# Moving stationary and moving tiles to other address differences modulo 512, and turning the order of three products in one stage

## The chip, the cores and the metric

The kernel runs on one core of a Trainium2 chip. The metric is the device time of one execution in microseconds. Before the change the median of two runs is 2041.47 us (2041.25 to 2041.7).

## What is computed

A decoder trunk of two layers for 256 tokens of width 2048, in float32, with 256 memory tokens. Cut to what matters:

```python
def layer_a(h, mem, ...):
    z = rms_norm(h, norm_attn) @ w_in                  # 2048 x (1536 + 1536 + 36 + 512)
    ... rope, native sparse attention (compressed, selected, window branches), memory attention
    h = h + concatenate([o_nsa, o_mem]) @ w_out        # 2048 x 2048
    return h + swiglu(rms_norm(h, norm_ffn), w_gate, w_up, w_down)   # d_ff = 5632

def reference(...):
    h = layer_a(x, mem, ...)
    kv = rms_norm(h, kv_norm) @ w_kv_shared            # 2048 x 1024
    ... layer_b: z = rms_norm(h, norm_attn) @ w_in     # 2048 x 2048
    ... dilated attention on the shared K and V, memory attention
    h = h + concatenate([o_dil, o_mem]) @ w_out        # 1024 x 2048
    h = h + swiglu(rms_norm(h, norm_ffn), w_gate, w_up, w_down)
    return rms_norm(h, final_norm)
```

`compress` in layer A's attention is a two-layer MLP over overlapping blocks of 32 tokens. The feed-forward parts are the largest matrix products.

## The kernel before

**Three products for one.** TensorE multiplies in the fp32r type. For accuracy each float32 operand is split into a high and a low part (`split`, lines 74 to 81: ScalarE makes the high part with a copy into fp32r, VectorE the low part as the difference). `mm3` then issues three matmuls into one PSUM tile: high by high (line 85), stationary low by moving high (line 86), stationary high by moving low (line 87). Its argument `l` is the stationary operand, 128 columns of activations that the array holds, and `r` the moving operand, up to 512 columns of weights that stream through. Each matmul instruction brings its own load of the stationary operand (LDWEIGHTS).

**Where the operands come from.** `load_w` brings a weight chunk by DMA on SyncE's queue into `raw` (pool `wp`, four buffers) and splits it into `whi` and `wlo` (three buffers each). `Gemm.part` runs `mm3` over the chunk's slices for one of the two halves of the tokens. Activations are split in advance and stay in SBUF: `xhi`/`xlo` (pool `xp`) hold the normalised input of a projection, `ohi`/`olo` (pool `pa`) the memory tokens and later the attention's output in layer A, `obhi`/`oblo` (pool `pc`) the attention's output in layer B, `hThi`/`hTlo` (pool `h`) the hidden activations of the feed-forward part.

**The feed-forward part** (`Group`, `run_groups`) multiplies the first six row blocks of the contraction in a Strassen form: quarters of the weights are loaded into `q11`, `q12`, `q22`, `q21`, combined by VectorE, split into `qhi` and `qlo` (pool `q`) and used by `product`; the other row blocks come as plain chunks through `load_w` (`plain`). So both `w` and `q` weights meet `x` (gate and up) and `hT` (down).

**Order.** TensorE's order is the order of the program text. `Side.tick` puts the smaller steps (transposes, attention products) between the slices of the large products at hand-written places. The other engines' order is left to the framework.

**Stages in time.** Memory K/V of both layers (stationary `o`), layer A's projections (stationary `x`, two of them in blocks of 274 columns), layer A's attention among its query projection, output projection (`o`), layer A's feed-forward part, layer B's shared K/V and query projections with its attention (`x`), output projection (`ob`), layer B's feed-forward part.

**Where tiles lie.** A pool's tiles stand one after the other, each buffer rounded up to 32 bytes per partition, and pools that are open together stand one after the other in the order of opening: constants, `wp`, `xp`, `small`, `work`, and then those of the phase (in layer A `ac`, `pa`, `p1` or `p2`; in the feed-forward phases `h` and `q`; in layer B's attention `acb` and `pc`). Some tiles exist only to move what follows (`padc`, `padw`, `pada`). Laid out so, `whi`, `wlo`, `xhi`, `xlo`, `ohi`, `olo`, `obhi`, `oblo`, `hThi`, `hTlo`, `qhi` and `qlo` all begin 224 bytes beyond a multiple of 512, and a 128-column slice of fp32r is 512 bytes long. So before the change every matmul with 512 columns has its stationary and its moving tile at difference 0 modulo 512. A slice of 274 columns is 1096 bytes, 72 beyond a multiple of 512, so in those blocks every second slice has another difference. In the compression MLP (lines 624 and 625) the stationaries are 60 columns, 240 bytes apart.

Of the kernel before, what the change touches and what calls it, by code (L numbers as in the profile page):

```python
# [8 lines left out]
F32 = mybir.dt.float32  # L9
# [7 lines left out]
P = 128  # L17
# [24 lines left out]
def decoder_trunk(ctx: ExitStack, tc: tile.TileContext, a: dict, out: bass.AP):  # L42
    nc = tc.nc

    const = ctx.enter_context(tc.tile_pool(name="const", bufs=1))
    wp = ctx.enter_context(tc.tile_pool(name="wp", bufs=4))
    dram = ctx.enter_context(tc.tile_pool(name="dram", bufs=1, space=bass.MemoryType.DRAM))
    xp = ctx.enter_context(tc.tile_pool(name="xp", bufs=1))
    small = ctx.enter_context(tc.tile_pool(name="small", bufs=6))
    work = ctx.enter_context(tc.tile_pool(name="work", bufs=1))  # L50
    work.tile([P, 20], F32, name="padw")
    phase = ctx.enter_context(ExitStack())
    aux_stack = ExitStack()
    fbufs = [1]
    fpool = mm_ps = aux_ps = mm_tags = None

    def open_phase(name, mms, auxs):
        nonlocal mm_ps, mm_tags, aux_ps
        mm_ps = phase.enter_context(tc.tile_pool(name="m" + name, bufs=1, space=PSUM))
        mm_tags = mms  # L60
        phase.enter_context(aux_stack)
        aux_ps = aux_stack.enter_context(tc.tile_pool(name="x" + name, bufs=auxs, space=PSUM))
# [17 lines left out]
            nc.vector.scalar_tensor_tensor(lo, src, gain, hi.bitcast(F32),  # L80
                                           op0=ALU.mult, op1=ALU.subtract)

    def mm3(o, l, r, start, stop, more=False):

        nc.tensor.matmul(o, l[0], r[0], start=start, stop=False, skip_group_check=more)  # L85
        nc.tensor.matmul(o, l[1], r[0], start=False, stop=False, skip_group_check=more)  # L86
        nc.tensor.matmul(o, l[0], r[1], start=False, stop=stop, skip_group_check=more)  # L87

    def pair(f):
        return f(0), f(1)  # L90
# [38 lines left out]
    class Gemm:  # L129
# [16 lines left out]
        def part(self, ws, tt, k0, side):  # L146
            for i, w in enumerate(ws):
                k = k0 + i
                x = self.xs[k](tt)
                mm3(self.ps[tt][:, :self.ncols], x, w, k == 0, k == self.nk - 1)  # L150
                side.tick()

    def cols(pr):
# [2 lines left out]
    def take(steps=()):  # L156
        got = deferred + list(steps)
        deferred.clear()
        return Side(got)

    def at(fs, *ticks):
        assert len(fs) == len(ticks)
        return list(zip(ticks, fs))
# [4 lines left out]
    def gemm(chunks, xs, ncols, nk, gain=None, steps=(), pre=None, first=None):  # L168
        side = take(steps)
        g = Gemm(chunks, xs, ncols, nk, gain)  # L170
        g.run(0, len(chunks), side, pre, first)
        side.flush()
        return g.ps

    def wblocks(name, nb, nchunk):
        w = a[name]
        return [[w[b, c] for c in range(nchunk)] for b in range(nb)]
# [27 lines left out]
    def finish_rstd(ssq, n):  # L205
        v = small.tile([P, 2], F32, tag="var", name="var")
        if n > 1:
            nc.vector.tensor_reduce(v, ssq, axis=AX.X, op=ALU.add)
        else:
            nc.vector.tensor_copy(v, ssq[:, :, 0])  # L210
        nc.vector.tensor_scalar(v, v, 1.0 / D, EPS, op0=ALU.mult, op1=ALU.add)
        r = small.tile([P, 2], F32, tag="rstd", name="rstd")
        nc.gpsimd.tensor_tensor(r, v, halfneg, op=ALU.pow)
        return r
# [5 lines left out]
    def new_ssq():  # L220
        return small.tile([P, 2, 4], F32, tag="ssq", name="ssq")
# [12 lines left out]
    def new_x():  # L234
        return pair(lambda i: xp.tile([P, XW], F32R, tag=("xhi", "xlo")[i], name=("xhi", "xlo")[i]))
# [85 lines left out]
    def residual_block(ps, nb, ssq, op, ticks=(3, 5)):  # L321
        for tt in range(2):
            hb = h[:, tt, nb * 512:(nb + 1) * 512]
            nc.vector.tensor_add(hb, ps[tt], hb)
            square_sum(ssq[:, tt, nb:nb + 1], hb)
        deferred.extend(at([lambda k2=k2: op.turn(nb, k2) for k2 in range(2)], *ticks))
# [66 lines left out]
    def mem_head(q, mkT, mv, hd, O):  # L393
        st = {}

        def scores():
            S = aux_tile()
            for qt in range(2):
                mm3(S[:, qt * T:(qt + 1) * T], sl(q, slice(None), slice(qt * P, (qt + 1) * P)),
                    sl(mkT, slice(None), hd, slice(None)), True, True)  # L400
            negm = small.tile([P, 2], F32, tag="mnegm", name="mnegm")
            den = small.tile([P, 2], F32, tag="mden", name="mden")
            nc.vector.tensor_reduce(negm, S.rearrange("p (q k) -> p q k", q=2), axis=AX.X, op=ALU.max, negate=True)
            E = new_E(512)
            for qt in range(2):
                exp_(E[:, qt * T:(qt + 1) * T], S[:, qt * T:(qt + 1) * T], negm[:, qt:qt + 1], den[:, qt:qt + 1])
            c = softmax_coef(den)
            for qt in range(2):
                nc.vector.tensor_scalar_mul(E[:, qt * T:(qt + 1) * T], E[:, qt * T:(qt + 1) * T], c[:, qt:qt + 1])
            st["E"] = E  # L410

        def turn():
            st["PT"] = new_PT("mPT")
            transposed([st["E"][:, qt * T + mt * P:qt * T + (mt + 1) * P] for mt in range(2) for qt in range(2)], st["PT"])

        def values():
            for mt in range(2):
                mm3(O(), sl(mv, slice(None), mt, slice(hd * P, (hd + 1) * P)),
                    sl(st["PT"], slice(None), slice(mt * T, (mt + 1) * T)), mt == 0, mt == 1)

        return scores, turn, values
# [20 lines left out]
    stack = ExitStack()  # L442
    pa = stack.enter_context(tc.tile_pool(name="pa", bufs=1))
    kv4 = [pa.tile([P, 1152], F32R, tag="kv4", name="kv4", bufs=4) for _ in range(4)]
    mkT_b = pair(lambda i: kv4[i][:, :1024].rearrange("p (c t) -> p c t", t=T))
    mv_b = pair(lambda i: kv4[2 + i][:, :1024].rearrange("p (c t) -> p c t", t=512))
    memkv = [dram.tile([P, 1024], F32, name=f"memkv{i}") for i in range(4)]
# [364 lines left out]
    def project_out(name, nk, ready, gi):  # L812
        op = Paired(new_x(), KT, lambda k: gains[:, gi, k:k + 1])
        ssq = new_ssq()
        ob = wblocks(name, 4, nk // CK)
        n = nk // CK
        side = take()
        g = [Gemm(ob[i], osx, 512, nk) for i in range(2)]
        side.rate = max(1, 8 / (2 * ready))
        for i in range(2):  # L820
            g[i].run(0, ready, side)
        side.flush()
        for i in range(2):
            side = take()
            g[i].run(ready, n, side)
            side.flush()
            residual_block(g[i].ps, i, ssq, op)
        for nb in range(2, 4):
            ps = gemm(ob[nb], osx, 512, nk)
            residual_block(ps, nb, ssq, op, (3, 5) if nb == 2 else (4, 10))  # L830
        return op, finish_rstd(ssq, 4)
# [198 lines left out]
    def open_ffn(name):  # L1030
        nonlocal fh, fq, fpool
        fbufs[0] = 2
        open_phase(name, FFN, 1)
        fh = phase.enter_context(tc.tile_pool(name="h" + name, bufs=1))
        fpool = fq = phase.enter_context(tc.tile_pool(name="q" + name, bufs=1))

    fh = fq = None
    open_ffn("fa")
    xb = None
    ssq_b = new_ssq()  # L1040
# [10 lines left out]
    phase.close()  # L1051

    open_phase("b", ATT, 4)
    ac = phase.enter_context(tc.tile_pool(name="acb", bufs=1))
    cs = ac.tile([P, 2, 2, HD], F32, name="cs")
    nc.gpsimd.dma_start(cs, a["cs"])
# [85 lines left out]
    for j in range(4):  # L1142
# [8 lines left out]
        deferred.extend(at(heads_T(tok, qT), 4, 7))  # L1151
        deferred.extend(at(dil_head(qT, j), 10, 13, 15, 20, 22, 25, 28, 30))
    fpool = pc
    fx, f_r = project_out("b_w_out", 8, 3, 6)
    stack.close()
    phase.close()
    open_ffn("fb")

    def final(db, hs, n):
# [137 lines left out]
def build(nc, arrays):  # L1297
    from concourse import tile as _tile

    aps = {}  # L1300
    import numpy as np
    for name, v in arrays.items():
        dt = BF16 if v.dtype.itemsize == 2 else mybir.dt.from_np(v.dtype)
        aps[name] = nc.dram_tensor(f"in_{name}_dram", v.shape, dt, kind="ExternalInput").ap()
    out = nc.dram_tensor("out_0_dram", (T, D), F32, kind="ExternalOutput").ap()
    with _tile.TileContext(nc) as tc:
        with tc.manual_schedule(engines={mybir.EngineType.PE}):
            decoder_trunk(tc, aps, out)
# [12 lines left out]
```

## Time and profile before

| | |
|---|---|
| Median of the runs | 2041.47 us |
| The profiled execution | 2041.91 us, span 2040.1 us |
| TensorE matmuls busy | 2020.5 us, 99%, 9417 instructions |
| Weight loads busy | 1676.7 us, 82%, 9417 instructions |
| VectorE busy | 1641.4 us, 80% |
| ScalarE busy | 1190.4 us, 58% |
| HBM read | 394.87 MB, 196 GB/s over the span |

Busy time of matmuls is a union of overlapping durations: one with 512 columns is shown with about 390 ns, while the next one starts much earlier. How fast TensorE goes is therefore read from the distance between starts in the timeline. PE is TensorE's matmul, PEld its weight load, DVE VectorE, ACT ScalarE, POOL GpSimd, SP SyncE. L85 is line 85 of the kernel; as `mm3` and `split` are helpers, the tile names tell which product a row belongs to.

### The profile page before, as it was taken

Reading aid. Unit: us, or ns where it says so; the run is one execution under the profiler, and the core shown is the slowest. Engines: PE = TensorE matmul, PEld = TensorE weight load, DVE = VectorE, ACT = ScalarE, POOL = GpSimd, SP = SyncE. Lnnn points to the kernel's source line nnn. Section 1 sums busy time; section 2 is a strip of 40 time slices with the busy share of each in tenths; the row PEclk is TensorE's granted clock in tenths of the full one; section 3 lists DMA queues with packets and bytes.
Section 4 is the critical chain, followed back from the end, with each engine's and each line's share of the span. In section 5 each row is a group of like instructions: output and inputs, shape, how many; then the busy total and the mean of one; then the engine's idle time right before and its main releaser. Section 6 shows DMA issues by size and latency. Waiting matters only on the chain.

```text
span 2040.1 us, 25602 instructions
## 1 busy us (share of the span) xinstructions
PE 2020.5 (99%) x9417; PEld 1676.7 (82%) x9417; DVE 1641.4 (80%) x2118; ACT 1190.4 (58%) x1573; POOL 10.8 (1%) x32
## 2 busy tenths in 40 slices
PE   9999999999999999999999999999999999999998
PEld 7898888878888888888887888878888888888886
DVE  6767898678888888888887678778888888888755
ACT  7755566656555566555565555656555565655543
POOL 0000000000000000000000000000000000000000
PEclk9999999999999999999999999999999999999999
DMA  8767633566655656556663755476556655566464
GB/s 302 270 201 236 218 116 122 178 253 199 208 184 194 201 195 225 186 186 208 203 209 114 235 167 158 147 262 201 185 186 201 225 202 186 182 206 221 136 204 146
DMA packets 104541, 400.74 MB, mean 196 GB/s; under 512 B 12128, under 2 KB 12512, under 8 KB 104032
## 3 DMA queue, kind: packets, MB, share of 16 engines
q1 hardware_dynamic: 103392, 395.31, 58.5%
q0 software_dynamic: 736, 2.75, 0.4%
q8 instruction: 74, 1.21, 0.3%
q10 hardware_dynamic: 288, 1.05, 0.1%
q14 instruction: 51, 0.42, 0.1%
HBM read 394.87 MB, written 4.19 MB: 196 GB/s over the span
## 4 chain that ended last, share of the span: by engine, by line
PE 95%; DVE 2%; ACT 1%; issue 0%; DMA 0%; SPq 0%; DVEq 0%; POOLq 0%; POOL 0%; ACTq 0%
PE mm L85 30%; PE mm L87 30%; PE mm L86 30%; PE aux L304 1%; PE aux L226 1%; DVE wlo L77 1%; PE aux L87 1%; PE aux L86 1%; PE aux L85 1%; PE aux L339 0%; ACT whi L76 0%; PE cmp L625 0%; PE cmp L624 0%; DVE E L377 0%; DMA memT_raw<-in_memT_dram 0%
## 5 line engine op out<-in xcount | busy, mean ns | idle before, releaser
L76 ACT ACTIVATE whi<-raw 128x1024 fp32r<-128x1024 f32 (+1 forms) x476 | 498.4, 1047 | 502.5 <-PE mm L86 461.3
L77 DVE TENSOR_TENSOR wlo<-raw,whi 128x1024 fp32r<-128x1024 f32 (+1 forms) x476 | 573.1, 1205 | 203.9 <-ACT whi L76 202.6
L85 PE MATMUL mm<-whi,xhi 128*128 128x512 f32 (+1 forms) x1376 | 537.5, 391 | 2.9 <-ACT junk L218 1.1
L87 PE MATMUL mm<-wlo,xhi 128*128 128x512 f32 (+1 forms) x1376 | 530.5, 386 | 0.0
L86 PE MATMUL mm<-whi,xlo 128*128 128x512 f32 (+1 forms) x1376 | 529.7, 385 | 0.0
L77 DVE TENSOR_TENSOR qlo<-q,qhi 128x1536 fp32r<-128x1536 f32 x210 | 368.6, 1757 | 75.5 <-ACT qhi L76 74.2
L76 ACT ACTIVATE qhi<-q 128x1536 fp32r<-128x1536 f32 x210 | 311.8, 1486 | 137.8 <-PE mm L86 115.2
L87 PEld LDWEIGHTS mm<-wlo,xhi 128*128 128x128 f32 x1376 | 258.3, 188 | 52.6
L85 PEld LDWEIGHTS mm<-whi,xhi 128*128 128x128 f32 x1376 | 258.6, 188 | 51.0 <-issue 2.5
L86 PEld LDWEIGHTS mm<-whi,xlo 128*128 128x128 f32 x1376 | 258.8, 188 | 47.0
L85 PE MATMUL mm<-whi,hThi 128*128 128x512 f32 x464 | 182.0, 392 | 0.1
L86 PE MATMUL mm<-whi,hTlo 128*128 128x512 f32 x464 | 180.7, 389 | 0.9 <-DVE hTlo L77 0.9
L87 PE MATMUL mm<-wlo,hThi 128*128 128x512 f32 x464 | 180.8, 390 | 0.0
L87 PE MATMUL mm<-qlo,xhi 128*128 128x512 f32 x420 | 163.5, 389 | 0.0
L85 PE MATMUL mm<-qhi,xhi 128*128 128x512 f32 x420 | 163.5, 389 | 0.0
L86 PE MATMUL mm<-qhi,xlo 128*128 128x512 f32 x420 | 163.5, 389 | 0.0
L80 DVE SCALAR_TENSOR_TENSOR wlo<-raw,gains,whi 128x512 fp32r<-128x512 f32 x160 | 113.8, 747 | 47.0 <-ACT whi L79 46.8
L79 ACT ACTIVATE whi<-raw,gains 128x512 fp32r<-128x512 f32 x160 | 107.7, 716 | 58.9 <-PE mm L86 51.3
L85 PE MATMUL mm<-whi,ohi 128*128 128x512 f32 x256 | 102.7, 401 | 1.3 <-ACT whi L79 1.3
L86 PEld LDWEIGHTS mm<-whi,hTlo 128*128 128x128 f32 x464 | 87.2, 188 | 19.0 <-DVE hTlo L77 1.2
L85 PEld LDWEIGHTS mm<-whi,hThi 128*128 128x128 f32 x464 | 87.1, 188 | 18.1 <-ACT hThi L76 0.6
L87 PEld LDWEIGHTS mm<-wlo,hThi 128*128 128x128 f32 x464 | 87.1, 188 | 18.1
(279 smaller groups left out, 2480.0 us busy)
## 6 DMA issues: line engine op xcount, KB each, us to landing
raw<-in_a_gu_s_dram SPq DMA_DIRECT2D x100, 512.0 KB, 4.2
raw<-in_b_gu_s_dram SPq DMA_DIRECT2D x100, 512.0 KB, 3.6
q<-in_a_gu_q_dram SPq DMA_DIRECT2D x40, 768.0 KB, 5.4
q<-in_b_gu_q_dram SPq DMA_DIRECT2D x40, 768.0 KB, 5.7
raw<-in_a_dn_s_dram SPq DMA_DIRECT2D x52, 512.0 KB, 4.2
raw<-in_b_dn_s_dram SPq DMA_DIRECT2D x40, 512.0 KB, 4.3
q<-in_a_dn_q_dram SPq DMA_DIRECT2D x24, 768.0 KB, 5.7
raw<-in_a_w_out_dram SPq DMA_DIRECT2D x32, 512.0 KB, 3.6
```

What stands on the lines that cost most here:

```text
L76: nc.scalar.activation(hi, src, AF.Copy)
L77: nc.vector.tensor_sub(lo, src, hi.bitcast(F32))
L79: nc.scalar.activation(hi, src, AF.Copy, scale=gain)
L80: nc.vector.scalar_tensor_tensor(lo, src, gain, hi.bitcast(F32), op0=ALU.mult, op1=ALU.subtract)
L85: nc.tensor.matmul(o, l[0], r[0], start=start, stop=False, skip_group_check=more)
L86: nc.tensor.matmul(o, l[1], r[0], start=False, stop=False, skip_group_check=more)
L87: nc.tensor.matmul(o, l[0], r[1], start=False, stop=stop, skip_group_check=more)
L226: nc.tensor.transpose(ps[:, i * P:(i + 1) * P], s, ident)
L304: nc.tensor.transpose(ps[:, i * P:(i + 1) * P], tok[tt][:, i * P:(i + 1) * P], ident)
```

## The change

Five pad tiles are added or resized, and `mm3` gets an option for another order.

- `padx` (64 bytes) ahead of `wp`'s tiles moves `w` and `x` on by 64; `padw` shrinks from 80 bytes (96 with rounding) to 16 (32), so that everything from `work` on lies where it did.
- `pado` (32 bytes) ahead of `ohi` moves `o` on by 32.
- `padh` (256 bytes) moves `hT` on by 256, `padq` (256 bytes) moves `q` by another 256, in both feed-forward phases.
- `beside[0]` is true during layer B's shared K/V and query projections. There `Gemm.part` calls `mm3` with `turned=True`: high by high, then stationary high by moving low, then stationary low by moving high. Two matmuls with the same stationary operand stand side by side. Everywhere else the order is as before.

Start modulo 512 and the difference stationary minus moving, worked out from the tile sizes:

| family (stationary/moving) | starts before | after | difference before | after |
|---|---|---|---|---|
| x/w | 224, 224 | 288, 288 | 0 | 0 |
| o/w | 224, 224 | 256, 288 | 0 | -32 |
| ob/w | 224, 224 | 224, 288 | 0 | -64 |
| x/q | 224, 224 | 288, 224 | 0 | 64 |
| hT/w | 224, 224 | 480, 288 | 0 | 192 |
| hT/q | 224, 224 | 480, 224 | 0 | 256 |

```diff
     wp = ctx.enter_context(tc.tile_pool(name="wp", bufs=4))
+    wp.tile([P, 16], F32, name="padx", bufs=1)
...
-    work.tile([P, 20], F32, name="padw")
+    work.tile([P, 4], F32, name="padw")
...
     fbufs = [1]
+    beside = [False]
...
-    def mm3(o, l, r, start, stop, more=False):
-
-        nc.tensor.matmul(o, l[0], r[0], start=start, stop=False, skip_group_check=more)
-        nc.tensor.matmul(o, l[1], r[0], start=False, stop=False, skip_group_check=more)
-        nc.tensor.matmul(o, l[0], r[1], start=False, stop=stop, skip_group_check=more)
+    def mm3(o, l, r, start, stop, more=False, turned=False):
+
+
+        prods = ((0, 0), (0, 1), (1, 0)) if turned else ((0, 0), (1, 0), (0, 1))
+        for n, (i, j) in enumerate(prods):
+            nc.tensor.matmul(o, l[i], r[j], start=start and n == 0, stop=stop and n == 2, skip_group_check=more)
...
-                mm3(self.ps[tt][:, :self.ncols], x, w, k == 0, k == self.nk - 1)
+                mm3(self.ps[tt][:, :self.ncols], x, w, k == 0, k == self.nk - 1, turned=beside[0])
...
     kv4 = [pa.tile([P, 1152], F32R, tag="kv4", name="kv4", bufs=4) for _ in range(4)]
+    pa.tile([P, 8], F32, name="pado")
...
         fh = phase.enter_context(tc.tile_pool(name="h" + name, bufs=1))
+        fh.tile([P, 64], F32, name="padh")
         fpool = fq = phase.enter_context(tc.tile_pool(name="q" + name, bufs=1))
+        fq.tile([P, 64], F32, name="padq")
...
     open_phase("b", ATT, 4)
+    beside[0] = True
...
     fpool = pc
+    beside[0] = False
     fx, f_r = project_out("b_w_out", 8, 3, 6)
```

## The prediction

> **What bounds the kernel now.** I read the page first: the engines' busy shares, the granted clock, the chain that ended last.
>
> ```profile
> span 2040.1 us, 25602 instructions
> PE 2020.5 (99%) x9417; PEld 1676.7 (82%) x9417; DVE 1641.4 (80%) x2118; ACT 1190.4 (58%) x1573; POOL 10.8 (1%) x32
> PEclk9999999999999999999999999999999999999999
> PE 95%; DVE 2%; ACT 1%; issue 0%; DMA 0%; SPq 0%; DVEq 0%; POOLq 0%; POOL 0%; ACTq 0%
> ```
>
> TensorE works through the whole span at the full granted clock, and 95% of the chain is its own instructions. So a gain or a loss must come from the distance between the starts of consecutive matmuls. The groups, with shapes kept apart, say which matmuls these are. Columns: line, engine, operation, output<-inputs, shape, count, busy us, mean ns of one, idle us before it.
>
> ```profile
> L85 PE MATMUL mm<-whi,xhi 128*128 128x512 f32 x1312 | 518.9, 396 | 2.9 <-ACT junk L218 1.1 <-ACT whi L76 0.9 <-DVE h L324 0.9
> L85 PE MATMUL mm<-whi,hThi 128*128 128x512 f32 x464 | 182.0, 392 | 0.1
> L85 PE MATMUL mm<-qhi,xhi 128*128 128x512 f32 x420 | 163.5, 389 | 0.0
> L85 PE MATMUL mm<-whi,ohi 128*128 128x512 f32 x256 | 102.7, 401 | 1.3 <-ACT whi L79 1.3
> L85 PE MATMUL mm<-qhi,hThi 128*128 128x512 f32 x210 | 81.9, 390 | 0.0
> L85 PE MATMUL mm<-whi,obhi 128*128 128x512 f32 x64 | 26.0, 407 | 0.0
> ```
>
> Lines 86 and 87 have the same counts, so `mm3` runs 2726 triples, 8178 matmuls with 512 columns. The 390 ns is latency; matmuls overlap. The price is the distance of starts, from the timeline in undisturbed stretches (first and last of each):
>
> ```profile
> 629.76 0.39 PE L85 MATMUL mm<-qhi,hThi 128*128 128x512 f32 x1
> ...
> 639.96 0.39 PE L85 MATMUL mm<-whi,hThi 128*128 128x512 f32 x1
> ...
> 1154.41 0.39 PE L85 MATMUL mm<-whi,xhi 128*128 128x512 f32 x1
> ...
> 1165.97 0.39 PE L85 MATMUL mm<-whi,xhi 128*128 128x512 f32 x1
> ```
>
> The first stretch holds 45 distances (down projection, q and w weights in turn): 10.20/45 = 0.2267 us. The second holds 51 (the stage that the change turns): 11.56/51 = 0.2267 us. By the layout told above both have address difference 0 modulo 512, and they agree to the last digit. 8178 x 0.2267 = 1854 us, 91% of the span. One nanosecond on all of them would be 8.2 us.
>
> **The pads.** They add no instruction. They change the difference (stationary minus moving, modulo 512) of these families: o/w to -32 (256 triples), x/q to +64 (420), hT/w to +192 (464), hT/q to +256 (210), ob/w to -64 (64). That is 1414 triples, 4242 matmuls; x/w, the largest family, stays at 0. So the sum is 4242 times a price p per matmul that no 512-column row of before shows: 4.24 us per nanosecond. I bound p by the nearest rows that have other differences.
>
> First, the 274-column blocks. A weight chunk there holds two slices of 274 columns, 1096 bytes, so triples alternate between difference 0 (first slice) and -72 (second, 72 bytes beyond a multiple of 512). Only line 85, the head of each triple, is shown; the triple that starts at 111.66 is a first slice:
>
> ```profile
> 111.27 0.29 PE L85 MATMUL mm<-whi,xhi 128*128 128x274 f32 x1
> ...
> 111.66 0.29 PE L85 MATMUL mm<-whi,xhi 128*128 128x274 f32 x1
> ...
> 112.04 0.29 PE L85 MATMUL mm<-whi,xhi 128*128 128x274 f32 x1
> ...
> 112.41 0.29 PE L85 MATMUL mm<-whi,xhi 128*128 128x274 f32 x1
> ...
> 112.79 0.29 PE L85 MATMUL mm<-whi,xhi 128*128 128x274 f32 x1
> ...
> 113.17 0.29 PE L85 MATMUL mm<-whi,xhi 128*128 128x274 f32 x1
> ...
> 113.55 0.29 PE L85 MATMUL mm<-whi,xhi 128*128 128x274 f32 x1
> ...
> 113.93 0.29 PE L85 MATMUL mm<-whi,xhi 128*128 128x274 f32 x1
> ...
> 114.30 0.29 PE L85 MATMUL mm<-whi,xhi 128*128 128x274 f32 x1
> ```
>
> Difference 0: 0.38 + 0.38 + 0.38 + 0.37 = 1.51 us for 12 matmuls, 125.8 ns each. Difference -72: 0.39 + 0.37 + 0.38 + 0.38 = 1.52, 126.7 ns. Leaving 0 costs about +0.8 ns here.
>
> Second, the compression MLP, whose stationaries are 240 bytes apart, so that the difference walks through many values. One step of eight matmuls and what follows it:
>
> ```profile
> 162.90 0.28 PE L624 MATMUL cmp<-whi,cx 128*60 128x256 f32 x1
> ...
> 163.37 0.28 PE L624 MATMUL cmp<-whi,cx 128*60 128x256 f32 x1
> ...
> 163.82 0.40 PE L85 MATMUL mm<-whi,xhi 128*128 128x512 f32 x1
> ...
> 164.98 0.39 PE L87 MATMUL mm<-wlo,xhi 128*128 128x512 f32 x1
> ```
>
> The first four distances (differences 0 and 240) average 0.47/4 = 117.5 ns, the next four (480 and 208) 0.45/4 = 112.5 ns. The address difference, or something that goes with it, moves a matmul by 5 ns. Then the 512-column matmuls right behind it, at difference 0, take 1.16/5 = 232 ns each, 5 ns over the steady 226.7.
>
> So p lies between -5 and +5 ns, that is -21 to +21 us. For the forecast I take the 274-column row, +0.8 ns, because its stationaries are full 128-column tiles in long steady runs, as in the families that move: 4242 x 0.8 = +3.4 us. The compression's stationaries have 60 columns and its runs are eight long, so it gives the bounds only.
>
> A rule of the Trainium skill speaks against the pads. "TensorE: Matmul & The Clock Gate", section "Step-by-step: what each phase is for", says that TensorE reads the moving operand and the weights through two independent SBUF ports. By that rule p would be 0 and the sum 0. The 5 ns of the compression rows do not follow from it; no row here with 512 columns tests it.
>
> **The turned stage.** Layer B's 64 + 128 = 192 triples (shared K/V, then queries) now go (xhi, whi), (xhi, wlo), (xlo, whi). The number of instructions stays. Could the second weight load be dropped or hidden better? The compression already runs two matmuls on one stationary, line 624 and then 625:
>
> ```profile
> L624 PEld LDWEIGHTS cmp<-whi,cx 128*60 128x60 f32 x64 | 8.4, 131 | 0.6
> L625 PEld LDWEIGHTS cmp<-wlo,cx 128*60 128x60 f32 x64 | 8.4, 131 | 2.0 <-DVE wlo L77 0.5
> ```
>
> 64 matmuls on each line and 64 loads: nothing is dropped, and the load takes 131 ns both times. So I put the gain at 0; bounds: 192 pairs by 5 ns either way, 1 us.
>
> What the turn can cost is a wait. wlo is now wanted 0.227 us after whi instead of 0.453 us. ACT makes whi, DVE makes wlo from it. In the stage, who waited for whom:
>
> ```profile
> PEld mm L85 <- ACT whi L79: 1.5, 1, 1.5
> PE mm L85 <- ACT junk L218: 1.1, 1, 1.1
> ```
>
> These are the stage's only waits of the main matmuls on a fresh tile or a sum; none names wlo. The cover is the three buffers: a chunk lasts 12 matmuls, 12 x 0.2267 = 2.72 us, and weights are split two chunks ahead. Behind a waiting matmul stands all of TensorE, so without that cover the 48 chunks would cost 48 x 0.227 = 11 us. In the other direction, whi's buffer comes free one matmul later (its last reader is now third) and wlo's one earlier; ACT would begin its next split 0.23 us later, hidden by the same lead. Value: 0.
>
> **The sum.** Profiled execution 2041.9 us (span 2040.1 and 1.8 around it), +3.4 + 0 = 2045.3. The median of the runs, 2041.5, is 0.4 lower: 2044.9 us.
>
> **The rivals.**
>
> *No pace change at all.* The 0.2267 us could be fixed per matmul wherever the operands lie (two ports), or the unwritten pad tiles might not shift anything: 2041.5. For it: the same pace in families whose tiles lie in different pools. Against: all of those have difference 0, and the compression rows vary. It lies inside the forecast's case.
>
> *The pads lift a conflict (faster).* At difference 0 the weight load for the next matmul and the moving stream start together on the same address modulo 512; if they hinder each other, moving apart saves what the cheaper compression half shows, 5 ns: 2041.5 - 21 = 2020. For it: 512 columns take 226.7 ns while 240 and 208 of difference show that such spans can shrink. Against: the 274-column rows go the other way. Over 2% (40.8 us) would need 9.6 ns on every one of the 4242. Beside this stands the rule in the same page of the Trainium skill, section "Back-to-back issue gap": a warm matmul's distance is about N/2.4 + 2.5 ns, 215.7 ns at 512 columns. The trace does not agree, 226.7. Lifting all 11 ns of that from 4242 matmuls would be an estimate of -47 us, 1995.
>
> *The pads make one (slower).* The steady 226.7 ns is then the state in which load and stream keep clear of each other, and the other differences hold the matmuls in the 232 ns state seen behind the compression step: 4242 x 5.3 = +22 us, 2064. For it: the sign of the 274-column rows, and that 5 ns is what a disturbed 512-column run shows. Against: that run falls back to 226.7 by itself, and its own difference was 0. It decides from about +2.4 ns on; over 2% needs 9.6 ns, twice anything seen.
>
> **How the numbers follow.** Forecast's case, p within about 2.4 ns of 0 either way, with the no-change rival in it: 0.65, own range 2031 to 2055. Faster rival 0.14, of which a quarter goes beyond 2%. Slower rival 0.21, of which 0.07 goes beyond 2%: the least known families (+192, +256) are the large ones. Two per cent, 41 us, is about what a measurement of this kernel can tell from no change; below 2000.6 is 0.03, above 2082.3 is 0.07, the rest 0.90. The range takes both rivals to their prices with some room above, 2018 to 2070, and leaves out their tails.
>
> **What would show it.** In the profile after: the distances by family. x/q, hT/w, hT/q, o/w and ob/w within 2.4 ns of 226.7, with x/w still at 226.7, carries the forecast; one family at 232 or more, or at 222 or less, is a rival at that difference. The turned stage should keep its 0.2267 us, with as many loads as matmuls and no wait on wlo. I would be wrong if the differences differ among themselves by more than 5 ns, or if TensorE begins to wait in the turned stage.

## The result, and the profile after

The changed kernel takes 2065.94 us (median of two runs, 2064.24 to 2067.65) where the kernel before takes 2041.47. The ratio is 1.012, with a 95% interval of 1.008 to 1.016: slower by 24.5 us, a clear loss, though under 2%. The profiled execution took 2067.65 us (span 2065.8), so its span is 25.7 us longer than that of before.

The page after, the same lines as before the change: span, busy shares, granted clock, and shares of the chain that ended last.

```profile
span 2065.8 us, 25600 instructions
PE 2042.4 (99%) x9417; PEld 1676.9 (81%) x9417; DVE 1643.8 (80%) x2118; ACT 1190.1 (58%) x1573; POOL 10.8 (1%) x32
PEclk9999999999999999999999999999999999999999
PE 95%; DVE 2%; DMA 1%; ACT 1%; issue 1%; SPq 0%; POOLq 0%; POOL 0%; ACTq 0%; DVEq 0%
```

Nothing has become a bound that was none: the same 9417 matmuls, the same clock, TensorE still 95% of the chain (DMA's 1% comes up below). It is only busy 21.9 us longer. The groups by shape (`mm3` now stands on line 90) give no more than a hint:

```profile
L90 PE MATMUL mm<-whi,xhi 128*128 128x512 f32 x1312 | 520.7, 397 | 2.9 <-DVE h L327 2.0 <-ACT whi L78 0.9
L90 PE MATMUL mm<-whi,hThi 128*128 128x512 f32 x464 | 184.1, 397 | 0.1
L90 PE MATMUL mm<-qhi,xhi 128*128 128x512 f32 x420 | 165.6, 394 | 0.0
```

The mean of one matmul is up by 1 to 5 ns, but that is latency, and the idle time before the groups is unchanged. What was lost shows in the distance between starts. The timeline of the memory K/V stage (start us, duration, engine, line, operation), first before and then after, the same 57 distances of the o/w family, which moved from difference 0 to -32:

```profile
35.68 0.39 PE L85 MATMUL mm<-whi,ohi 128*128 128x512 f32 x1
...
48.60 0.39 PE L85 MATMUL mm<-whi,ohi 128*128 128x512 f32 x1
```

```profile
35.90 0.40 PE L90 MATMUL mm<-whi,ohi 128*128 128x512 f32 x1
...
49.20 0.39 PE L90 MATMUL mm<-whi,ohi 128*128 128x512 f32 x1
...
502.42 0.39 PE L90 MATMUL mm<-qhi,xhi 128*128 128x512 f32 x1
...
504.52 0.39 PE L90 MATMUL mm<-whi,xhi 128*128 128x512 f32 x1
...
506.35 0.39 PE L90 MATMUL mm<-wlo,xhi 128*128 128x512 f32 x1
...
507.26 0.39 PE L90 MATMUL mm<-whi,xhi 128*128 128x512 f32 x1
...
509.98 0.39 PE L90 MATMUL mm<-qhi,xhi 128*128 128x512 f32 x1
...
645.68 0.40 PE L90 MATMUL mm<-whi,hThi 128*128 128x512 f32 x1
...
650.48 0.39 PE L90 MATMUL mm<-whi,hThi 128*128 128x512 f32 x1
```

- o/w at -32: 13.30/57 = 0.2333 us after, 12.92/57 = 0.2267 before.
- x/q at 64 (502.42 to 504.52): 2.10/9 = 0.2333 us.
- x/w, still at 0, right behind it (504.52 to 506.35): 1.83/8 = 0.2288. Some way on (507.26 to 509.98): 2.72/12 = 0.2267, the old pace. After a family at another difference it takes x/w about ten matmuls to come back to it.
- hT/w at 192 (645.68 to 650.48): 4.80/21 = 0.2286.

The same over the whole trace, worked out from the starts of all 512-column matmuls. The means are of the distances up to 300 ns from one 512-column matmul to the next; the right column is the difference of the family's whole time, after minus before.

| family | difference | matmuls | ns before | ns after | us |
|---|---|---|---|---|---|
| x/q | 0 to 64 | 1260 | 227.0 | 233.3 | +7.9 |
| o/w | 0 to -32 | 768 | 227.6 | 233.2 | +4.2 |
| hT/w | 0 to 192 | 1392 | 227.0 | 229.5 | +3.4 |
| hT/q | 0 to 256 | 630 | 227.2 | 229.9 | +1.7 |
| ob/w | 0 to -64 | 192 | 229.7 | 230.8 | +0.2 |
| x/w, distances up to 300 ns | 0 | 3936 | 227.7 | 228.6 | +2.9 |
| x/w, distances over 300 ns | 0 | | | | +5.7 |

The families that moved cost 17.4 us, 4.1 ns for each of the 4242 matmuls. The attention's value products (tile `V`) moved by the way and cost 0.2; the transposes cost 0.4 less. With the x/w rows that makes 25.8 us; the spans differ by 25.7.

One of these means hides two paces. hT/q, at 256, is slow only behind another family. In one of its longest stretches, 18 matmuls behind x/w, it is back at the old pace from the fourth on:

```profile
1056.93 0.39 PE L90 MATMUL mm<-qhi,hThi 128*128 128x512 f32 x1
...
1060.33 0.39 PE L90 MATMUL mm<-whi,xhi 128*128 128x512 f32 x1
```

3.40/15 = 0.2267 us. In a second stretch of 18, behind hT/w, it is back after ten. hT/w at 192 doesn't come back: in its stretches of 24 it stays at about 229.

Of the 5.7 us in long x/w distances, 3.4 stand at two places, the starts of the feed-forward parts. The chain of waits in order of time and the timeline show the first:

```profile
421.70 7.18 DMA q<-in_a_gu_q_dram
```

```profile
432.79 1.09 PE L229 MATMUL aux<-ident,h 128*128 128x128 f32 x4 [2.71 <-DVE xlo L82]
```

The first quarter of the gate weights is late, and TensorE stands 2.71 us before it can transpose. From the matmul ahead to this transpose it is 3102 ns here and 861 before; in layer B 1931 and 803. The experiments show whether that belongs to the change.

### The profile page after: what moved, and what is told of

Same layout as the page of the kernel before. It is cut to its first block, busy times and chain, and to the rows that moved or that the text cites. A ratio compares the mean times of both kernels' runs of the same rounds, so it can differ in the third digit from the quotient of the medians.

```text
span 2065.8 us, 25600 instructions
## 1 busy us (share of the span) xinstructions
PE 2042.4 (99%) x9417; PEld 1676.9 (81%) x9417; DVE 1643.8 (80%) x2118; ACT 1190.1 (58%) x1573; POOL 10.8 (1%) x32
## 4 chain that ended last, share of the span: by engine, by line
PE 95%; DVE 2%; DMA 1%; ACT 1%; issue 1%; SPq 0%; POOLq 0%; POOL 0%; ACTq 0%; DVEq 0%
PE mm L90 89%; PE aux L90 2%; PE aux L307 1%; PE aux L229 1%; DVE wlo L79 1%; PE aux L342 0%; DMA q<-in_a_gu_q_dram 0%; PE cmp L629 0%; PE cmp L628 0%; DMA q<-in_b_gu_q_dram 0%; DVE E L380 0%; DMA raw<-in_a_w_q_dram 0%; ACT qhi L78 0%; DMA memT_raw<-in_memT_dram 0%; ACT whi L78 0%
```

## The experiments

Three questions: which half of the change costs, whether it is the difference or the moved tiles as such, and what other differences cost. Where an interval is given, the kernel was timed against the kernel before on the same chip.

**The turn alone.** From the changed kernel, all pads taken back:

```diff
-    wp.tile([P, 16], F32, name="padx", bufs=1)
-    work.tile([P, 4], F32, name="padw")
+    work.tile([P, 20], F32, name="padw")
-    pa.tile([P, 8], F32, name="pado")
-        fh.tile([P, 64], F32, name="padh")
-        fq.tile([P, 64], F32, name="padq")
```

> The kernel before with the turned order in layer B's K/V and query projections and no new pad. Theory D (the distance of matmul starts depends on the difference stationary minus moving modulo 512, and nothing else changed the time): 2041.5 us, 0.2267 us in the turned stage. Theory T (the turn has a share in the 24 us): 2045 or more, and the turned stage slower than before.

Measured: 2041.56 us against 2041.35, ratio 0.9998 (0.9989 to 1.0008). The timeline of the turned stage:

```profile
1177.84 0.39 PE L89 MATMUL mm<-whi,xhi 128*128 128x512 f32 x1
...
1179.88 0.39 PE L89 MATMUL mm<-whi,xhi 128*128 128x512 f32 x1
```

2.04/9 = 0.2267 us. The turn alone does nothing, either way.

**The pads alone.**

```diff
-    beside[0] = True
+    beside[0] = False
```

> The changed kernel with the old order of products everywhere. Theory D: 2066 us as the changed kernel, x/q at 233 ns, hT/q 230, hT/w 229.5, o/w 233. Theory T: several us below 2066.

Measured: 2064.6 us, ratio 1.011 (1.009 to 1.013). By family x/q 233.3 ns, o/w 233.3, hT/w 229.5, hT/q 229.9, the same as after. The whole loss is the pads'.

**All moved, by 512.** From the kernel before, one pad made 512 bytes larger, so that every tile from `work` on (`o`, `ob`, `hT`, `q`) lies elsewhere and every difference stays 0 modulo 512:

```diff
-    work.tile([P, 20], F32, name="padw")
+    work.tile([P, 148], F32, name="padw")
```

> The kernel before with one pad larger by 512 bytes, so that o, hT, q and ob all move by 512 against w and x, and every difference is 0 modulo 512 again. Theory D with 512 as its period: 2041.5 us and 226.7 ns in every family. If the period is longer (1024, 2048), or if it is the moved tiles themselves that cost (they lie over other tiles of the stage before, and the feed-forward part's first loads wait longer): above 2045, with 4 us more at the starts of the feed-forward parts.

Measured: 2042.35 us, ratio 1.000 (0.999 to 1.001). The timeline of its x/q products, now 512 bytes apart:

```profile
504.04 0.39 PE L85 MATMUL mm<-qhi,xhi 128*128 128x512 f32 x1
...
506.08 0.39 PE L85 MATMUL mm<-whi,xhi 128*128 128x512 f32 x1
```

2.04/9 = 0.2267 us. Moving tiles costs nothing; their difference modulo 512 does. This kernel's profiled execution has the late load too, in its chain of waits and its timeline:

```profile
417.09 6.62 DMA q<-in_a_gu_q_dram
```

```profile
427.61 1.08 PE L226 MATMUL aux<-ident,h 128*128 128x128 f32 x4 [2.19 <-DVE xlo L80]
```

TensorE stands 2.19 us at the same place, with all differences 0. So the late load doesn't need other differences. It comes and goes: the turn alone has 765 ns there, and a kernel with all the pads (the turn everywhere, below) has 986.

**One tile moved.** From the kernel before, only `q` is moved, so that x/q and hT/q stand at 64 while x/w, hT/w and o/w stay at 0:

```diff
+        fq.tile([P, 112], F32, name="padq")
```

> The kernel before with only the q tiles moved, x/q and hT/q both at difference 64, everything else at 0. Theory D: x/q and hT/q at 233 ns, that is 1890 matmuls by 6.4 ns = +12 us, and x/w and hT/w, which stand between them at difference 0, slower by 1.5 ns on 2784 because each return to difference 0 takes about ten matmuls to settle, +4 us: 2057 us. If x/w's loss in the changed kernel had another cause: 2053, with x/w at 227.0. If the value goes by the stationary's family and not by the difference: hT/q at 230 ns.

Measured: 2058.45 us, ratio 1.008 (1.006 to 1.010).

```profile
500.73 0.39 PE L85 MATMUL mm<-qhi,xhi 128*128 128x512 f32 x1
...
502.83 0.39 PE L85 MATMUL mm<-whi,xhi 128*128 128x512 f32 x1
...
504.21 0.39 PE L85 MATMUL mm<-whi,xhi 128*128 128x512 f32 x1
...
505.57 0.39 PE L85 MATMUL mm<-qhi,xhi 128*128 128x512 f32 x1
```

x/q at 64: 2.10/9 = 0.2333 us; x/w behind it, at 0: 1.38/6 = 0.230, then 1.36/6 = 0.2267. Over the trace x/q costs 7.9 us more, hT/q (233.2 ns) 3.8, and the two families that did not move 2.9 (x/w) and 1.3 (hT/w): 15.9 us, where the spans of the two profiled executions differ by 15.7 and the medians by 17.1. hT/q takes 233.2 ns at 64 and 229.9 at 256, so the price goes with the difference, not with the tile. And what did not move pays a fifth of the bill (4.2 of 15.9), because it alternates with what did.

**Other differences.** Three more kernels, made from the kernel before, each with three pads of its own sizes (`pado`, `padh`, `padq`); the first is

```diff
+    pa.tile([P, 24], F32, name="pado")
+        fh.tile([P, 32], F32, name="padh")
+        fq.tile([P, 88], F32, name="padq")
```

with 72, 24, 48 columns in the second and 104, 8, 32 in the third.

> A look at five other differences: x/q 32, o/w 96, hT/w 128, hT/q 160, x/w and ob/w 0. Theory D: each family has its own distance of starts, between 226.7 and 236 ns; if 0 is the best difference there is, none is below 226.7, and the time lies between 2050 and 2070 us. If some difference lets the weight load and the stream pass each other without loss, its family comes near 216 ns and the time falls below 2041.

> As the run before, with x/q 224, o/w 288, hT/w 96, hT/q 320. Theory D: hT/w at 96 has the same distance of starts as o/w at 96 in the run before, within 1 ns; none below 226.7 if 0 is the best.

> As the two runs before, with x/q 352, o/w 416, hT/w 32, hT/q 384. Theory D: hT/w at 32 as x/q at 32 two runs before, within 1 ns; none below 226.7 if 0 is the best.

Measured: 2067.4, 2074.9 and 2068.5 us, with 2040.8 for the kernel before beside them. The o/w stretch that was shown above, in the first of them (difference 96):

```profile
35.75 0.39 PE L85 MATMUL mm<-whi,ohi 128*128 128x512 f32 x1
...
49.10 0.39 PE L85 MATMUL mm<-whi,ohi 128*128 128x512 f32 x1
```

13.35/57 = 0.2342 us. The mean distances by difference, from these three and the kernels above (16 is from a kernel further down):

| difference modulo 512 | ns |
|---|---|
| 0 | 226.7 to 227.0 |
| 16 | 226.7 |
| 32, 64, 96 | 233.0, 233.3, 234.1 |
| 128, 160 | 232.8, 233.9 |
| 192 | 229.5 |
| 224 | 233.3 |
| 256 | 229.9 (226.7 once settled) |
| 288, 320, 352 | 233.2, 233.7, 233.6 |
| 384, 416 | 232.2, 233.3 |
| 480 | 233.2 |

Where two families had the same difference they agree within 0.2 ns (96: o/w 234.1, hT/w 233.9; 32: x/q and hT/w 233.0; 64: x/q 233.3, hT/q 233.2). None of the others is below 0's. (448, -64, is left out: only ob/w had it, whose stage is disturbed and shows 229.7 ns already at 0.)

**Which read meets which?** `mm3` uses three stationary tiles in turn: high, low, high. A matmul's own stationary was loaded before it starts, and the next one's is loaded while it streams (a load takes 188 ns, and starts are 226.7 ns apart). Moving only one of the two tiles separates the two. First `xlo` alone, to 64:

```diff
-    work.tile([P, 20], F32, name="padw")
+    work.tile([P, 4], F32, name="padw")
-        return pair(lambda i: xp.tile([P, XW], F32R, tag=("xhi", "xlo")[i], name=("xhi", "xlo")[i]))
+        xhi = xp.tile([P, XW], F32R, tag="xhi", name="xhi")
+        xp.tile([P, 16], F32, tag="padl", name="padl")
+        return xhi, xp.tile([P, XW], F32R, tag="xlo", name="xlo")
```

> The kernel before with xlo alone moved by 64 bytes against xhi and the weights. In a triple the first matmul (xhi) streams at difference 0 while the load of xlo, at 64 from that stream, goes on beside it; the second (xlo) streams at its own difference 64 while xhi's load, at 0 from the stream, goes on. Theory N (the load of the next stationary and the stream hinder each other): the distance behind the first matmul grows to about 233 ns, those behind the second and third stay at 227. Theory O (a matmul's own difference counts): the second's grows, the first and third stay. Either way about 1732 matmuls by 6.4 ns = +11 us, more if each change of difference unsettles the next ones.

Then `xhi` alone, to 64, with `xlo` at 0:

```diff
-        return pair(lambda i: xp.tile([P, XW], F32R, tag=("xhi", "xlo")[i], name=("xhi", "xlo")[i]))
+        xp.tile([P, 16], F32, tag="padh0", name="padh0")
+        xhi = xp.tile([P, XW], F32R, tag="xhi", name="xhi")
+        xp.tile([P, 112], F32, tag="padl", name="padl")
+        return xhi, xp.tile([P, XW], F32R, tag="xlo", name="xlo")
```

> The mirror of the run with xlo moved: now xhi lies at 64 from w and q, and xlo at 0. If the own difference of a matmul counts: the distances behind the first and the third matmul of a triple (stationary xhi) are about 233 to 236 ns, the one behind the second (xlo) 227 to 229. If the difference between the stream and the load that goes on beside it counts: slow are the second (its stream goes beside the load of xhi, at 64) and the third (beside the next xhi), and the first is near 227. Time about 2041 + 3464 matmuls by 6.4 ns = 2063 us in both.

Measured: 2066.2 us for the first and 2066.55 for the second, each in one run. The first is 24 us over the kernel before, where both theories gave 11; 5.6 of them are x/w distances over 300 ns. The distance behind each matmul of an x/q triple, mean over the trace:

| kernel | high by high | low by high | high by low |
|---|---|---|---|
| `xlo` at 64 | own 0, next 64: 229.0 | own 64, next 0: 235.4 | own 0, next 0: 228.5 |
| `xhi` at 64 | own 64, next 0: 232.6 | own 0, next 64: 233.3 | own 64, next 64: 230.8 |

The first kernel alone says that the matmul's own stationary is what counts. The second says no: its middle matmul has its own at 0 and is slow. "The next load" explains that one, but not the 235.4 of the first kernel. All three distances rise in both, also where own and next are 0. Neither rule holds by itself, and it stays open which read meets which.

The kernel with `xhi` moved shows another thing. Its timeline in layer A's projection, 274 columns, and in the feed-forward part, 512:

```profile
108.02 0.29 PE L85 MATMUL mm<-whi,xhi 128*128 128x274 f32 x1
...
117.89 0.29 PE L85 MATMUL mm<-whi,xhi 128*128 128x274 f32 x1
...
504.60 0.39 PE L85 MATMUL mm<-qhi,xhi 128*128 128x512 f32 x1
...
506.70 0.39 PE L85 MATMUL mm<-whi,xhi 128*128 128x512 f32 x1
```

274 columns: 26 triples, 9.87/78 = 126.5 ns; before it was (114.30 - 111.27)/24 = 126.3, from the rows in the prediction. Apart by slices and over the whole trace, the first ones (0 before, two matmuls of three at 64 now) go from 125.5 to 126.5 ns, the second ones (-72 before, two of three at -8 now) stay within 0.1 of 126.8. 512 columns: 2.10/9 = 233.3 ns in this stretch, 232.2 over all q triples, against 227.0. With the same tile moved by the same 64 bytes the 274-column matmuls change by about 1 ns and the 512-column ones by more than 5.

Two things keep this from being a price by number of columns. In the 274-column blocks the difference changes with every triple, so no stretch there has one difference for the ten matmuls that x/w takes to settle. And their distances also shift where neither `x` nor `w` moved: in the first of the three kernels under other differences the first slices take 128.6 ns and the second 124.8, in the second 128.0 and 125.3. Over both slices the mean is 126.1 ns before and between 126.0 and 127.2 in every kernel here.

**The valley around 0.** `xhi` and `xlo` both at 16, by slices that begin 4 columns into wider tiles (`padw` gives the room back):

```diff
-    work.tile([P, 20], F32, name="padw")
+    work.tile([P, 16], F32, name="padw")
...
+        xhi = xp.tile([P, XW + 128], F32R, tag="xhi", name="xhi")
+        xlo = xp.tile([P, XW + 8], F32R, tag="xlo", name="xlo")
+        return xhi[:, 4:4 + XW], xlo[:, 4:4 + XW]
```

> The kernel before with xhi and xlo moved by 16 bytes against w and q, half the smallest step tried. If 0 itself is the best difference: x/w and x/q at 230 to 234 ns, 5196 matmuls by 3 to 6 ns, 2057 to 2073 us. If there is a valley around 0: 226.7 ns and 2041. If its floor lies beside 0: below 2041.

Measured: 2041.56 us in one run, with 2041.83 for the kernel before beside it.

```profile
501.47 0.39 PE L85 MATMUL mm<-qhi,xhi 128*128 128x512 f32 x1
...
503.51 0.39 PE L85 MATMUL mm<-whi,xhi 128*128 128x512 f32 x1
```

2.04/9 = 0.2267 us: 16 is as good as 0 and no better. Between 16 and 32 the price begins.

**The turn everywhere, with the pads.** Perhaps two matmuls on one stationary side by side save something only where the difference isn't 0:

```diff
-    beside = [False]
+    beside = [True]
-    def mm3(o, l, r, start, stop, more=False, turned=False):
+    def mm3(o, l, r, start, stop, more=False, turned=True):
-    beside[0] = False
```

> The changed kernel with the turned order everywhere, also where the difference is not 0. Theory D (the order does not matter): 2066 us, or a little more where the feed-forward part now wants the low weights earlier. If two matmuls with the same stationary do save something away from difference 0: one of three distances in x/q, hT/w, hT/q and o/w falls toward 226.7, 1350 of them by 3 to 6 ns, 2058 to 2062 us.

Measured: 2064.04 us, ratio 1.011 (1.009 to 1.013), as with the pads alone. The distance between two matmuls on the same stationary is no shorter than the others: x/q 233.1 against 233.4, o/w 233.3 against 233.1, hT/w 231.4 against 228.7. That hT/w figure goes with the place in the triple: behind the first matmul it is 231.4 in the old order too (the pads alone), behind the second 227.6 and behind the third 229.7 or 229.8, whichever tiles these are.

No kernel here is faster than the one before. Its layout, all differences 0, is the best one measured.

## Why the prediction was right or wrong

**What bounds the kernel: right.** The loss is in the distance between starts; busy shares, clock, chain and idle times hardly changed.

**The pads: right in form, wrong in size.** "4242 times a price p" is how the loss is built, but p was taken as +0.8 ns, for +3.4 us. Measured, p is 6.3 ns (x/q), 5.7 (o/w), 2.5 (hT/w), 2.7 (hT/q) and 1.1 (ob/w); over all 4242 it is 4.1 ns, 17.4 us. The step that failed is the choice between the bounds: the 274-column row was preferred "because its stationaries are full 128-column tiles in long steady runs". Those runs are long but not steady: their difference changes with every triple, and a 512-column family takes about ten matmuls to settle after such a change. Over the whole trace before, the two slices lie 1.4 ns apart (125.5 and 126.8), not 0.8, and that too would have given only 5.9 us. With `xhi` at 64 the first slices go from 125.5 to 126.5 ns while 512 columns go from 227.0 to 232.2, so the row could not show what a 512-column matmul pays. Whether that is for its shorter matmuls or for its changing differences isn't separated: no kernel here has 274 columns at one difference. The upper bound of +5 ns, from the 512-column matmuls behind the compression, was the nearer number; x/q and o/w go beyond it.

**A term was missing: x/w.** It was said to stay, since its difference stays 0. It pays all the same where it alternates with a family at another difference. Within the feed-forward parts its mean goes from 227.0 to 228.6 ns (layer A) and 228.4 (layer B), some 4 us on 2784 matmuls. (The table's 2.9 is less: the other stages took back 0.3, and four distances in layer A's part stand among those over 300 ns after the change, 0.9.) With only `q` moved, x/w loses 2.9 us and hT/w 1.3 at difference 0. The prediction had read the disturbed 512-column run behind the compression as a bound for p. That it falls back after some matmuls was the sign of this term: over all 16 compression steps of the trace before, the first two distances behind a step are 233.9 and 233.3 ns on average, and the eleventh, where so many follow, is 226.6. There are many changes of family in a feed-forward part.

**The slower rival: its price was near, its mechanism right in part.** It gave 5.3 ns and 2064 us. That this comes so close to 2065.94 is partly luck: the families that move pay 17.4 us and not 22, and x/w and the late loads happen to make up the rest. x/q and o/w do stay at 233.3 for as long as they last, so the other differences hold the matmuls at a slower pace, as it said. But hT/w and hT/q (2022 matmuls) pay less than half of that, and what hT/q pays at 256 is a wake that passes.

**No pace change, and the two ports.** The rule of the Trainium skill ("TensorE: Matmul & The Clock Gate", section "Step-by-step: what each phase is for") that moving operand and weights come through two independent ports would have made p 0. The runs disagree: with nothing but `q`'s place changed, x/q goes from 227.0 to 233.3 ns. By whatever ports the two are read, they aren't independent of each other's addresses here.

**The faster rival: refuted as far as tried.** Its 5 ns would need a difference below 226.7 ns; of the fifteen others that were tried none is. The 216 ns that "Back-to-back issue gap" in the same page of the Trainium skill gives for 512 columns appear as the mean of no 512-column family of any run.

**The turned stage: right.** 0 was said, and 0 is measured (2041.56 against 2041.35 with the turn alone). Nor did a wait on `wlo` appear, and no load is dropped. In the trace after, who waited for whom in layer B's stage, and its weight loads by shape:

```profile
PEld mm L90 <- ACT whi L81: 1.5, 1, 1.5
PE mm L90 <- DVE h L327: 1.1, 1, 1.1
```

```profile
L90 PEld LDWEIGHTS mm<-wlo,xhi 128*128 128x128 f32 x192 | 36.1, 188 | 6.5
L90 PEld LDWEIGHTS mm<-whi,xhi 128*128 128x128 f32 x192 | 36.1, 188 | 7.9 <-ACT whi L81 1.5
L90 PEld LDWEIGHTS mm<-whi,xlo 128*128 128x128 f32 x192 | 36.0, 188 | 7.8
```

The two waits are as long as those of before (the second is put down to `h` on VectorE here, to `junk` on ScalarE before), and none names `wlo`. 192 loads stand for 192 matmuls in each row, the ones that repeat the stationary of the matmul ahead too.

**What would show it.** x/q and o/w, over 232, carry the slower rival at 64 and -32; hT/w and hT/q lie 2.8 and 3.2 ns above 226.7, outside the forecast's 2.4; ob/w's rise of 1.1 is inside, though its mean of 230.8 is not, nor was its 229.7 before. The moved families differ among themselves by 3.8 ns (229.5 to 233.3), and by 6.6 with 0 among them, so the text's condition for being wrong, more than 5 ns, is met once 0 is counted. What happened is the slower rival at its price, not the likeliest case.

**The late loads.** The 3.4 us at the starts of the feed-forward parts were in no part of the prediction. They occur with all differences 0 and are missing in one kernel with all the pads, so they aren't a price of the differences. Whether they come more often with the pads, and why the load is late in some executions, was not tried and stays open.

## What to carry to other kernels

When a kernel is a stream of matmuls at one distance, look at where stationary and moving tiles start: here a difference of 0 or 16 modulo 512 gave 226.7 ns for 512 columns, as did 256 once settled, and the others up to 234, so a few bytes of padding ahead of a pool were worth 1% with not one instruction changed. When you bound a price by a nearby row, ask first whether that row could show the price at all: the 274-column blocks change their difference with every triple, and barely moved in any kernel here. And count what alternates with the moved work as touched too, even if nothing about it changes.

## What the runs showed of the hardware

- The distance between 512-column fp32r matmuls, each with its own load of 128 columns, depends on the difference of the two tiles' start addresses modulo 512: 226.7 ns at 0 and 16, 229.5 at 192, 229.9 at 256 on average but 226.7 in a long stretch, 232.2 to 234.1 at the others tried from 32 to 480. A shift by exactly 512 changes nothing (ratio 1.000).
- With `xhi` moved by 64, matmuls with 512 columns go from 227.0 to 232.2 ns; the 274-column blocks, whose difference changes with every triple, go from 126.1 to 126.7 over both slices. Which of the two makes their price small isn't shown.
- After a change from difference 64 to 0 the pace comes back over about ten matmuls: mean distances of 230.5, 231.2, 228.5, 227.6 and 227.6 ns for the first five pairs of x/w behind x/q, then 226.8. The same course stands behind the compression steps of the kernel before (233.9 and 233.3 ns at first, 226.6 at the eleventh), with the matmuls' own difference at 0. Why it takes so long isn't known.
- Two matmuls in a row on the same stationary gain nothing, at difference 0 (ratio 0.9998) or elsewhere.
